# Expert stage of a two-block transformer on one core: norms applied after the up projection, fetched rows transposed later, loads ahead in whole tiles

## The chip, the core and the metric

The kernel runs on one core of a Trainium2 chip. TensorE (PE in the profile, its weight loads PEld) multiplies matrices, VectorE (DVE), ScalarE (ACT) and GpSimd (POOL) work on elements, and SyncE (SP) issues most of the DMAs; the five run beside one another and wait for each other through semaphores. The metric is the device time of one execution in microseconds, the median of the runs.

## The reference, cut to what matters

The program computes a whole small model on 512 tokens of width 1024 (first a block with two layers, then a second block). The change touches only its last part, the mixture of experts. There are 32 experts; a router gives each token two of them with a gate weight:

```python
def hier_moe(h, ...):                       # h = rmsnorm(x) * norm2_g
    ...
    gates = jnp.sum(jax.nn.one_hot(e_idx, N_EXPERTS) * e_weight[..., None], axis=1)
    ...
        a = jnp.einsum('nd,edf->nef', hf, w_g[sl])        # 1024 -> 256
        u = jnp.einsum('nd,edf->nef', hf, w_u[sl])        # 1024 -> 256
        hid = jax.nn.silu(a) * u * gates[:, sl, None]
        out = out + jnp.einsum('nef,efd->nd', hid, w_d[sl])   # 256 -> 1024
```

`rmsnorm(x, g) = x * rsqrt(mean(x*x) + eps) * g`. The factor `rsqrt(...)` is one number per token, so it can be multiplied onto the token's row, or onto `a` and `u`, with the same result.

## The kernel before, in words

All data are float32. A product is made of three (or, in the experts' up projection, of two stacked) matmuls over a high and a low part of each operand; so every weight tile that arrives (`wraw`, `h`, `xh`/`xl` or `t`, 128x1024, 0.5 MB) is split: ACT casts the high part (`whi`, L260), DVE subtracts (`wlo`, L261). Weights come in one stream of such tiles in the order of use, through SP's queue (`load` L254, `load_to` L235, `load_halves` L242).

**Expert stage (`moe`, from L1408).** The router ranks each token within its two experts; an expert has 64 slots (`CAP`). Six weight tiles belong to an expert: four for gate and up, two for down. Token rows, already times the norm's gain but without the token's norm factor, lie in DRAM (`xr`). Experts are taken in blocks of four (`EB`); `take(e)` prepares block e while block e-4 is computed:

- `onehot` (`oh`, DVE L1601), eight small matmuls (`slot_cols`, L1364) and some short DVE instructions (`slot_rows`) give for each slot the token's row number and norm factor; `sr` (L1378) is the cast of the row numbers to integers. Its tile has two buffers, and the row numbers of the block before the last are still read by that block's scatter.
- `rows_in` (L1392): two gathers by GpSimd fetch 128 rows each into `rows` (two tiles).
- L1474: GpSimd multiplies both tiles by the norm factors.
- `rows_turn`: PE transposes them (L1401), ACT and DVE split them into `xs` (L1404, L1405), which has two buffers.

For each expert `expert_up` runs 16 matmuls (L1618) with the rows' high and low parts stacked on the partitions, ACT copies the lower half (`low`, L1620) and one matmul with `fold` (L1626) adds it to the upper; `expert_hidden` takes the silu (`hid`, ACT L1628) and the product (DVE L1629). One expert later `expert_turn` transposes `hid` (L1638) and splits it (`hh`), and `expert_down` multiplies (L267 to L269) into two banks. After two experts `add_rows` applies the gates (`y`, ACT L1532 for one half, DVE L1533 for the other), and GpSimd scatters the rows with an adding DMA into the output (L1535).

`take` is a generator; the main loop advances it by `next(coming, None)`, once before the down projection and once after `expert_hidden` (twice in the first expert of a block). Where its `yield`s stand decides behind which expert's work an instruction is written. Within that the framework's scheduler places instructions on each engine; an engine executes in order, so what stands first and waits holds up what follows.

Loads ahead: tile j goes to one of 26 places (`AHEAD`), in turn: 9 `wraw` tiles (`RING`), 4 tiles of the finished activations (`h`), 8 pairs of half tiles `xh`, `xl`, and 5 pairs of `t`. A half tile pair is two DMAs and two splits.

```python
                n = j % AHEAD - RING
                ...
                    self.ahead[j] = self.load_halves(j, [self.p_x.tile([128, T], F32, name=t) for t in ("xh", "xl")])
```

Of the kernel before, what the change touches and what calls it, by code (L numbers as in the profile page):

```python
# [9 lines left out]
F32 = mybir.dt.float32  # L10
F32R = mybir.dt.float32r
I32 = mybir.dt.int32
U8 = mybir.dt.uint8
AF = mybir.ActivationFunctionType
OP = mybir.AluOpType
# [7 lines left out]
T = NM + S  # L23
H2 = T // 2
NT = S // 128
# [17 lines left out]
CAP = 64  # L43
EB = 4
# [9 lines left out]
RING = 9  # L54
AHEAD = RING + 17
# [146 lines left out]
class Ker:  # L202
# [252 lines left out]
        return rb[:, :n], y  # L455

    def xpair(self, n=T):
        return (self.p_x.tile([128, T], F32R, name="xh")[:, :n], self.p_x.tile([128, T], F32R, name="xl")[:, :n])

    def xsplit(self, h, gname, n=T, first=lambda k: None):  # L460

# [780 lines left out]
    def route_begin(self):  # L1242
        nc = self.nc
        rc = self.tmp()
        self.rc = [rc[:, 0:288].rearrange("p (a b) -> p a b", a=8), rc[:, 288:416], rc[:, 416:452], rc[:, 452:496]]
        for t, name in zip(self.rc, ("w_r", "tri", "b_r", "rdesc")):
            nc.gpsimd.dma_start(t, self.a[name])
        self.lgp = self.psb()
        zero = self.tmp(144)
        nc.vector.memset(zero, 0.0)  # L1250
        nc.tensor.matmul(self.lgp[:, :144], self.ident, zero, start=True, stop=False, skip_group_check=True)
        self.xt = {j: self.tmp(512) if n == 7 else self.p_x.tile([128, T], F32, name=("xh", "xl")[n % 2])[:, :512]
                   for n, j in enumerate(XORDER)}
        self.xr = self.p_d.tile([S, D], F32, name="xr")
        self.ss, self.nr = None, 0

# [151 lines left out]
    def moe(self):  # L1408
# [3 lines left out]
        with ExitStack() as es:  # L1412
# [5 lines left out]
            gcol = pk.tile([128, 4, NEXP // 2, 8], F32R, name="gcol")  # L1418
            nc.vector.memset(gcol.bitcast(F32), 0.0)
            self.xg = [pk.tile([128, D], F32, name=f"rows{n}") for n in range(EB // 2)]  # L1420
            for t in self.xg:
                nc.gpsimd.memset(t, 0.0)
            gall = pk.tile([128, 4, NEXP], F32, name="gall")
# [37 lines left out]
            def take(e):  # L1461
                n = EB // 2
                oh = self.onehot(pe, rank[:, :, e:e + EB], iota)
                s = self.slot_cols(pe, oh, gcol, e, n, 0, 8 if e else 4)
                r, y = self.slot_rows(pe, s, n)
                for b in range(n):
                    self.rows_in(b, r[:, b:b + 1])
                if e == 0:
                    self.gating(pr, found, gall, gcol)
                    s = self.slot_cols(pe, oh, gcol, e, n, 4, 8)  # L1470
                places[e] = r, self.slot_gates(pe, s)
                yield
                for b in range(n):
                    nc.gpsimd.tensor_scalar(self.xg[b], self.xg[b], y[:, b:b + 1], None, op0=OP.mult)  # L1474
                    yield
                for b in range(n):
                    yield from self.rows_turn(b, bufs(e)[0][:, :, 2 * b:2 * b + 2])

            def fetch(j):

                n = j % AHEAD - RING
                if n < 0:
                    self.ahead[j] = self.load(j)
                elif n < 4:
                    self.ahead[j] = self.load_to(j, self.hp[n])
                elif n < 12:
                    self.ahead[j] = self.load_halves(j, [self.p_x.tile([128, T], F32, name=t) for t in ("xh", "xl")])
                else:
                    self.ahead[j] = self.load_halves(j, [self.tmp(512), self.tmp(512)])

# [7 lines left out]
            for e in range(NEXP + 1):  # L1498
                if e % EB == 0:
                    list(coming)  # L1500
                    coming = take(e + EB) if e + EB < NEXP else iter(())
                if e < NEXP:
                    def hu(j, e=e):
                        if e * 6 + j not in self.ahead:
                            fetch(e * 6 + j)
                        return self.hu(idx=e * 6 + j)

                    x2, h2 = bufs(e)
                    up = self.expert_up(e % 2, x2, e % EB, hu, lambda: e and self.expert_turn(e % 2 == 0, *last))
                else:  # L1510
                    self.expert_turn(e % 2 == 0, *last)
                next(coming, None)
                if e > 0:
                    f = e - 1
                    if f % 2 == 0:
                        py = [self.psb(), self.psb()]
                    self.expert_down(py, f % 2 == 0, f % 2 == 1, *last)
                    if f % 2:
                        self.add_rows(pe, py, places[f // EB * EB], f % EB // 2, out)
                if e < NEXP:  # L1520
                    last = self.expert_hidden(e % 2, up), h2, hu
                for _ in range(2 if e % EB == 0 else 1):
                    next(coming, None)
            self.more_raw = None
# [2 lines left out]
    def add_rows(self, pe, py, place, b, out):  # L1527

        nc = self.nc
        r, g = place  # L1530
        y = pe.tile([128, D], F32, name="y")
        nc.scalar.activation(y[:, :512], py[0], AF.Copy, scale=g[:, b:b + 1])  # L1532
        nc.vector.tensor_scalar(y[:, 512:], py[1], g[:, b:b + 1], None, op0=OP.mult)  # L1533

        nc.gpsimd.indirect_dma_start(out=out[:S], out_offset=bass.IndirectOffsetOnAxis(ap=r[:, b:b + 1], axis=0), in_=y, in_offset=None,  # L1535
                                     bounds_check=S - 1, oob_is_err=False, compute_op=OP.add)

    def overflow(self, pe, cmax, rank, gall, gcol, xs, hh, out):
# [3 lines left out]
        with tc.If(cnt > CAP):  # L1542
# [5 lines left out]
            with tc.For_i(0, NEXP, 1) as e:  # L1548
                with tc.For_i(CAP, S, CAP) as b:
# [1 line left out]
                    nc.vector.memset(oh[:, :, CAP:2 * CAP].bitcast(F32), 0.0)  # L1551
                    r, y = self.slot_rows(pe, self.slot_cols(pe, oh, gcol, 0, 1, 0, 4), 1)
                    self.rows_in(0, r)
                    nc.gpsimd.tensor_scalar(self.xg[0], self.xg[0], y, None, op0=OP.mult)
                    list(self.rows_turn(0, xs[0][:, :, 0:2]))
                    hu = lambda j: self.hu(idx=e * 6 + j)
                    up = self.expert_hidden(0, self.expert_up(0, xs[0], 0, hu)), hh[:2], hu
                    self.expert_turn(False, *up)
                    py = [self.psb(), self.psb()]
                    self.expert_down(py, True, True, *up)  # L1560
# [34 lines left out]
    def onehot(self, pe, rank, iota):  # L1595

        nc = self.nc
        n = rank.shape[-1]
        m = n * CAP
        oh = pe.tile([128, NT, EB * CAP], F32R, name="oh", bufs=1)  # L1600
        nc.vector.tensor_tensor(oh[:, :, :m].rearrange("p a (e c) -> p a e c", e=n), iota[:, None, None, :].to_broadcast([128, NT, n, CAP]),  # L1601
                                rank[:, :, :, None].to_broadcast([128, NT, n, CAP]), op=OP.is_equal)
        return oh
# [16 lines left out]
        nc.scalar.copy(low[CAP:], pa[CAP:])  # L1620
        return pa, low

    def expert_hidden(self, par, up):
        nc = self.nc
        pa, low = up
        nc.tensor.matmul(pa, self.fold, low, start=False, stop=True, skip_group_check=True)  # L1626
        hid = self.hids[par]
        nc.scalar.activation(hid[:CAP], pa[:CAP, :256], AF.Silu)  # L1628
        nc.vector.tensor_mul(hid[:CAP], hid[:CAP], pa[:CAP, 256:])  # L1629
        return hid  # L1630

    def expert_turn(self, second, hid, hh, hu):
# [516 lines left out]
```

## Time and profile before

| | |
|---|---|
| runs (3) | median 1864.43 us, 1859.45 to 1865.34 |
| profiled execution | 1857.01 us, span 1855.2 us |
| PE busy in the span | 1694.2 us (91%), mean granted clock 0.956 |
| DVE, ACT, POOL busy | 1108.9, 844.4, 138.9 us |
| read from HBM | 221.89 MB |
| expert stage, first gather to the end | 1439.06 to 1855.2 us |

PE's share over the span is high because of the dense layers, which fill the first three quarters. The expert stage has other limits and is read by itself. In a timeline row the first number is the start in microseconds from the span's start, the second the time from the first start to the last end in the row; a bracket says how long the engine stood idle before and what ended it.

### The profile page before, as it was taken

Reading aid. Unit: us, or ns where it says so; the run is one execution under the profiler, and the core shown is the slowest. Engines: PE = TensorE matmul, PEld = TensorE weight load, DVE = VectorE, ACT = ScalarE, POOL = GpSimd, SP = SyncE. Lnnn points to the kernel's source line nnn. Section 1 sums busy time; section 2 is a strip of 40 time slices with the busy share of each in tenths; the row PEclk is TensorE's granted clock in tenths of the full one; section 3 lists DMA queues with packets and bytes.
Section 4 is the critical chain, followed back from the end, with each engine's and each line's share of the span. In section 5 each row is a group of like instructions: output and inputs, shape, how many; then the busy total and the mean of one; then the engine's idle time right before and its main releaser. Section 6 shows DMA issues by size and latency. Waiting matters only on the chain. (4 is left out here: it accounts for less than half of the span.)

```text
span 1855.2 us, 26474 instructions
## 1 busy us (share of the span) xinstructions
PE 1694.2 (91%) x10298; PEld 1459.3 (79%) x10298; DVE 1108.9 (60%) x1966; ACT 844.4 (46%) x1425; POOL 138.9 (7%) x99
## 2 busy tenths in 40 slices
PE   8999999999999999999999999999998566677766
PEld 8989999999999999788888886777777444555544
DVE  7667674534343445534343457997676567777766
ACT  5465553423232334413232335533634466676665
POOL 0000000000000000000000000000000424122222
PEclk9999999999999998999999999998999788998888
DMA  5211023222222221232332343121137688778771
GB/s 179 68 57 58 12 62 107 92 91 90 89 89 90 91 91 57 85 98 91 96 97 91 109 134 92 59 77 48 30 121 278 227 278 299 261 261 278 263 245 20
DMA packets 82418, 229.98 MB, mean 124 GB/s; under 512 B 11608, under 2 KB 11664, under 8 KB 82288
## 3 DMA queue, kind: packets, MB, share of 16 engines
q1 hardware_dynamic: 76752, 217.80, 35.3%
q0 software_dynamic: 5536, 10.45, 2.5%
q8 instruction: 82, 1.34, 0.3%
q14 instruction: 48, 0.39, 0.1%
HBM read 221.89 MB, written 14.69 MB: 128 GB/s over the span
## 5 line engine op out<-in xcount | busy, mean ns | idle before, releaser
L260 ACT CAST whi<-wraw 128x1024 fp32r<-128x1024 f32 (+1 forms) x271 | 281.9, 1044 | 626.3 <-PE pm L290 293.3
L261 DVE TENSOR_TENSOR wlo<-wraw,whi 128x1024 fp32r<-128x1024 f32 (+1 forms) x271 | 328.3, 1216 | 41.6 <-ACT whi L260 32.1
L290 PE MATMUL pm<-xh,whi 128*128 128x264 f32 x976 | 202.6, 289 | 8.9 <-ACT whi L260 6.0
L290 PE MATMUL pm<-xh,wlo 128*128 128x264 f32 x976 | 201.1, 287 | 0.0
L290 PE MATMUL pm<-xl,whi 128*128 128x264 f32 x976 | 200.9, 287 | 0.0
L290 PE MATMUL ps<-xh,whi 128*128 128x512 f32 x472 | 192.1, 407 | 0.0
L290 PE MATMUL ps<-xh,wlo 128*128 128x512 f32 x472 | 186.2, 395 | 0.0
L290 PE MATMUL ps<-xl,whi 128*128 128x512 f32 x472 | 185.5, 393 | 0.0
L290 PEld LDWEIGHTS pm<-xh,whi 128*128 128x128 f32 x976 | 153.2, 191 | 10.0 <-ACT whi L260 6.0
L290 PEld LDWEIGHTS pm<-xh,wlo 128*128 128x128 f32 x976 | 152.9, 190 | 0.1
L290 PEld LDWEIGHTS pm<-xl,whi 128*128 128x128 f32 x976 | 152.6, 190 | 0.4 <-DVE xl L468 0.3
L1618 PE MATMUL ps<-wlo,xs 128*128 128x512 f32 x256 | 110.7, 432 | 25.1 <-DVE wlo L261 24.5
L290 PEld LDWEIGHTS ps<-xh,whi 128*128 128x128 f32 x472 | 89.3, 189 | 23.7 <-issue 1.8
L1618 PE MATMUL ps<-whi,xs 128*128 128x512 f32 x256 | 106.0, 414 | 1.9 <-ACT whi L260 1.9
L290 PEld LDWEIGHTS ps<-xh,wlo 128*128 128x128 f32 x472 | 89.0, 189 | 21.0
L290 PEld LDWEIGHTS ps<-xl,whi 128*128 128x128 f32 x472 | 89.4, 189 | 19.5 <-issue 0.5
L290 PE MATMUL pm<-ah,whi 128*128 128x264 f32 x512 | 104.1, 284 | 0.0
L290 PE MATMUL pm<-ah,wlo 128*128 128x264 f32 x512 | 104.0, 285 | 0.0
L290 PE MATMUL pm<-al,whi 128*128 128x264 f32 x512 | 103.7, 284 | 0.0
L290 PE MATMUL ps<-ah,whi 128*128 128x512 f32 x256 | 101.1, 395 | 0.0
L290 PE MATMUL ps<-ah,wlo 128*128 128x512 f32 x256 | 101.0, 394 | 0.0
L290 PE MATMUL ps<-al,whi 128*128 128x512 f32 x256 | 100.5, 392 | 0.0
(499 smaller groups left out, 3277.6 us busy)
## 6 DMA issues: line engine op xcount, KB each, us to landing
wraw<-in_stream_dram SPq DMA_DIRECT2D x268, 512.0 KB, 3.5
t<-in_stream_dram SPq DMA_DIRECT2D x70, 256.0 KB, 5.5
h<-in_stream_dram SPq DMA_DIRECT2D x29, 512.0 KB, 5.5
xh<-in_stream_dram SPq DMA_DIRECT2D x56, 256.0 KB, 5.4
xl<-in_stream_dram SPq DMA_DIRECT2D x56, 256.0 KB, 5.5
h<-in_xT_dram SPq DMA_DIRECT2D x16, 264.0 KB, 3.5
hd<-h SPq DMA_DIRECT2D x8, 256.0 KB, 2.0
h<-hd SPq DMA_DIRECT2D x8, 256.0 KB, 3.5
```

The lines of the kernel that those rows point to most:

```text
L260: self.nc.scalar.copy(hi, src)
L261: i = self.nc.vector.tensor_sub(lo, src, hi.bitcast(F32))
L290: nc.tensor.matmul(ps, w[:, b, :], x[:, sl], start=(first and f and i == 0), stop=(last and l and i == nb - 1))
L1618: nc.tensor.matmul(pa, xk, v[:, k], start=kk == 0 and n == 0, stop=kk == 7 and n == 1, skip_group_check=True)
```

## The change

The scaling on GpSimd goes. The norm factor, brought to one column per expert (`sn`; for the second expert of a pair by eight narrow matmuls with the one-hot moved by 64 slots), becomes the scale of the silu and the scalar of the product. The transposes are written five yields behind the gathers in place of one yield and two scalings, so they stand in the third and fourth expert of the block before. Both halves of `y` are on ACT. `xh` and `xl` become the halves of one tile `xp`, into which a whole weight tile is loaded with one DMA; after the first 26 tiles the turn is over 21 places, without `t`. The one-hot tile moves to another pool.

```diff
     def xpair(self, n=T):
-        return (self.p_x.tile([128, T], F32R, name="xh")[:, :n], self.p_x.tile([128, T], F32R, name="xl")[:, :n])
+        t = self.p_x.tile([128, 2, T], F32R, name="xp")
+        return t[:, 0, :n], t[:, 1, :n]
...
             def take(e):
...
-                r, y = self.slot_rows(pe, s, n)
+                r, t = self.slot_rows(pe, s, n)
                 for b in range(n):
                     self.rows_in(b, r[:, b:b + 1])
+
+                y = pe.tile([128, EB], F32, name="sn")
+                y2 = y.rearrange("p (b two) -> p b two", two=2)
+                nc.vector.tensor_copy(y2[:, :, 0], t)
+                ps = self.psb()
+                for b in range(n):
+                    for i in range(NT):
+                        c = oh[:, i, b * 128 + CAP:min(b * 128 + CAP + 128, EB * CAP)]
+                        nc.tensor.matmul(ps[:c.shape[-1], b * 8:b * 8 + 4], c, gcol[:, i, e // 2 + b, :4],
+                                         start=i == 0, stop=i == NT - 1, skip_group_check=True)
+                s2 = pe.tile([128, n, 2], F32, name="sq")
+                nc.vector.tensor_copy(s2[:CAP], ps[:CAP, :n * 8].rearrange("p (a b) -> p a b", a=n)[:, :, 1:3])
+                nc.vector.tensor_add(y2[:CAP, :, 1], s2[:CAP, :, 0], s2[:CAP, :, 1])
...
-                yield
-                for b in range(n):
-                    nc.gpsimd.tensor_scalar(self.xg[b], self.xg[b], y[:, b:b + 1], None, op0=OP.mult)
+                places[e] = r, self.slot_gates(pe, s), y
+                for _ in range(5 if e else 1):
                     yield
                 for b in range(n):
                     yield from self.rows_turn(b, bufs(e)[0][:, :, 2 * b:2 * b + 2])
...
-                n = j % AHEAD - RING
+                n = (j if j < AHEAD else (j - AHEAD) % (AHEAD - 5)) - RING
...
                 elif n < 12:
-                    self.ahead[j] = self.load_halves(j, [self.p_x.tile([128, T], F32, name=t) for t in ("xh", "xl")])
+                    self.ahead[j] = self.load_to(j, self.p_x.tile([128, 2, T], F32, name="xp"))
...
     def add_rows(self, pe, py, place, b, out):
...
         nc.scalar.activation(y[:, :512], py[0], AF.Copy, scale=g[:, b:b + 1])
-        nc.vector.tensor_scalar(y[:, 512:], py[1], g[:, b:b + 1], None, op0=OP.mult)
+        nc.scalar.activation(y[:, 512:], py[1], AF.Copy, scale=g[:, b:b + 1])
...
-    def expert_hidden(self, par, up):
+    def expert_hidden(self, par, up, y):
...
-        nc.scalar.activation(hid[:CAP], pa[:CAP, :256], AF.Silu)
-        nc.vector.tensor_mul(hid[:CAP], hid[:CAP], pa[:CAP, 256:])
+        nc.scalar.activation(hid[:CAP], pa[:CAP, :256], AF.Silu, scale=y)
+        nc.vector.scalar_tensor_tensor(hid[:CAP], pa[:CAP, 256:], y, hid[:CAP], op0=OP.mult, op1=OP.mult)
```

What stands on the engines, at the border between the second and the third block (experts 8 and 9; `hid` of expert 8 and then of expert 9). DVE before, from the scatter's second `y` half to the first `xs` of the rows that `sr` names:

```order
L1533 TENSOR_SCALAR y<-ps,sg 128x512
L1629 TENSOR_TENSOR hid_13315<-hid_13315,ps 64x256
L1386 TENSOR_TENSOR sg<-sp 64x2 x2
L261 TENSOR_TENSOR wlo<-wraw,whi 128x1024
L261 TENSOR_TENSOR hh_13304<-ps,hh_13301 128x2x64
L261 TENSOR_TENSOR wlo<-wraw,whi 128x1024 x2
L1378 CAST sr<-st 128x2
L261 TENSOR_TENSOR wlo<-wraw,whi 128x1024 x3
L1629 TENSOR_TENSOR hid_13319<-hid_13319,ps 64x256
L1601 TENSOR_TENSOR oh<-iota,rank 128x1024
L1405 TENSOR_TENSOR xs_13306<-ps,xs_13306 128x4x2x64
```

DVE now, at the same border, from expert 8's `hid` to the first `xs`:

```order
L1645 SCALAR_TENSOR_TENSOR hid_13256<-ps,sn,hid_13256 64x256
L261 TENSOR_TENSOR wlo<-h_91,whi 128x1024
L261 TENSOR_TENSOR wlo<-h_92,whi 128x1024
L1382 CAST sr<-st 128x2
L261 TENSOR_TENSOR hh_13245<-ps,hh_13242 128x2x64
L261 TENSOR_TENSOR wlo<-wraw,whi 128x1024 x2
L261 TENSOR_TENSOR wlo<-xp,whi 128x1024 x3
L1645 SCALAR_TENSOR_TENSOR hid_13260<-ps,sn,hid_13260 64x256
L261 TENSOR_TENSOR wlo<-xp,whi 128x1024
L261 TENSOR_TENSOR wlo<-h_93,whi 128x1024
L261 TENSOR_TENSOR hh_13250<-ps,hh_13248 128x2x64
L1409 TENSOR_TENSOR xs_13247<-ps,xs_13247 128x4x2x64
```

`y` has left DVE, the one-hot has moved ahead of `sr` (just above the first row shown), and seven splits stand between `sr` and the first `xs`, where three stood.

PE before, at the same place: the last matmuls of expert 9's up projection, its `fold`, the transposes of the first fetched tile, then the down projection of expert 8 (`hh`):

```order
L1618 MATMUL ps<-whi,xs_13306 128x512
L1618 MATMUL ps<-wlo,xs_13306 128x512
L1626 MATMUL ps<-low_13318,fold 128x512
L1401 MATMUL ps<-c_97,rows_13295 128x128 x4
L267 MATMUL ps<-whi,hh_13301 128x512
L268 MATMUL ps<-wlo,hh_13301 128x512
L269 MATMUL ps<-whi,hh_13304 128x512
```

PE now, in the up projection of expert 10, behind the turn of expert 9 (L1654); the down projection of expert 8 lies further up:

```order
L1633 MATMUL ps<-wlo,xs_13244 128x512
L1654 MATMUL ps<-c_97,hid_13260 128x128 x2
L1633 MATMUL ps<-whi,xs_13244 128x512
L1405 MATMUL ps<-c_97,rows_13235 128x128 x4
L1633 MATMUL ps<-wlo,xs_13244 128x512
L1633 MATMUL ps<-whi,xs_13244 128x512
L1633 MATMUL ps<-wlo,xs_13244 128x512
L267 MATMUL ps<-whi,hh_13248 128x512 x2
```

The transposes have moved behind the down projection of expert 8 and half of expert 10's up projection.

What `sr` waits for is the same in both; DVE before, with waits (DMASW are the semaphores of the DMAs that GpSimd issues, DMAHW of those that SP issues):

```order
L261 TENSOR_TENSOR wlo<-wraw,whi 128x1024 [waits DMAHW2_49]
L261 TENSOR_TENSOR wlo<-wraw,whi 128x1024 [waits DMAHW3_49]
L1378 CAST sr<-st 128x2 [waits DMASW6_49,DMASW7_49,DMASW5_49,DMASW4_49]
L261 TENSOR_TENSOR wlo<-wraw,whi 128x1024 [waits DMAHW4_49,PE_49,Activation_49]
L261 TENSOR_TENSOR wlo<-wraw,whi 128x1024 [waits DMAHW5_49,PE_49,Activation_49]
```

In the changed program `sr` (L1382) waits for the same four semaphores; only its neighbours have moved.

## Rows read from the trace of the kernel before

**Rows 1.** The page's forty slices of the span (46.4 us each), busy tenths of PE and DMA.

```profile
PE   8999999999999999999999999999998566677766
...
DMA  5211023222222221232332343121137688778771
```

**Rows 2.** Windows of about one block, cut at the gathers: length, busy us (and instructions) of PE, PEld, DVE, ACT, POOL, granted clock, DMA share, GB/s.

```profile
1565.80:1617.10 51.30, 35.68 (x148) 26.06 (x148) 36.50 (x59) 32.89 (x55) 13.26 (x6) 0.87 0.76 256
...
1667.00:1719.00 52.00, 36.90 (x147) 27.06 (x147) 36.21 (x59) 31.05 (x53) 13.04 (x7) 0.83 0.83 278
1719.00:1771.80 52.80, 37.81 (x149) 27.37 (x149) 36.83 (x58) 32.64 (x54) 12.97 (x6) 0.82 0.76 252
```

**Rows 3.** Who waited for whom from 1400 to 1855 us: total, times, longest.

```profile
PE ps L1401 <- POOL rows L1474: 73.7, 9, 11.9
...
DVE xs L1405 <- ACT xs L1404: 52.9, 11, 11.4
...
DVE sr L1378 <- issue: 27.3, 6, 5.6
...
DVE wlo L261 <- ACT whi L260: 23.4, 19, 2.3
```

**Rows 4.** GpSimd in order of time.

```profile
1446.25 5.69 POOL L1474 TENSOR_SCALAR rows<-rows,sy 128x1024 f32<-128x1024 f32 x2 [4.70 <-DMA rows<-xr,sr]
...
1504.51 1.56 POOL L1535 DMA_INDIRECT out_dram<-y,sr  x1 [15.86 <-DVE sg L1386]
...
1538.10 10.00 POOL L1535 DMA_INDIRECT out_dram<-y,sr  x1 [12.89 <-ACT whi L260]
1556.09 2.47 POOL L1535 DMA_INDIRECT out_dram<-y,sr  x1 [7.99 <-DVE sg L1386]
...
1570.75 2.85 POOL L1474 TENSOR_SCALAR rows<-rows,sy 128x1024 f32<-128x1024 f32 x1 [1.43 <-DMA rows<-xr,sr]
1574.66 2.84 POOL L1474 TENSOR_SCALAR rows<-rows,sy 128x1024 f32<-128x1024 f32 x1 [1.06 <-DMA rows<-xr,sr]
1589.67 1.90 POOL L1535 DMA_INDIRECT out_dram<-y,sr  x1 [12.16 <-DVE xs L1405]
...
1812.90 2.25 POOL L1535 DMA_INDIRECT out_dram<-y,sr  x1 [15.92 <-ACT whi L260]
```

**Rows 5.** DVE in order of time.

```profile
1473.68 0.69 DVE L1405 TENSOR_TENSOR xs<-ps,xs 128x512 fp32r<-128x512 f32 x1 [4.55 <-ACT xs L1404]
...
1533.63 1.22 DVE L261 TENSOR_TENSOR wlo<-h,whi 128x1024 fp32r<-128x1024 f32 x1
1534.76 1.28 DVE L1405 TENSOR_TENSOR xs<-ps,xs 128x512 fp32r<-128x512 f32 x2
...
1541.10 0.68 DVE L261 TENSOR_TENSOR wlo<-xh,whi 128x512 fp32r<-128x512 f32 x1
1541.70 0.68 DVE L261 TENSOR_TENSOR wlo<-xl,whi 128x512 fp32r<-128x512 f32 x1
...
1554.54 0.75 DVE L1533 TENSOR_SCALAR y<-ps,sg 128x512 f32<-128x512 f32 x1
1555.21 0.41 DVE L1629 TENSOR_TENSOR hid<-hid,ps 64x256 f32<-64x256 f32 x1
...
1564.79 0.17 DVE L1378 CAST sr<-st 128x2 int32<-128x2 f32 x1 [4.98 <-issue]
...
1575.42 0.69 DVE L1405 TENSOR_TENSOR xs<-ps,xs 128x512 fp32r<-128x512 f32 x1 [5.55 <-ACT xs L1404]
1578.44 1.22 DVE L261 TENSOR_TENSOR wlo<-h,whi 128x1024 fp32r<-128x1024 f32 x1 [2.33 <-ACT whi L260]
1580.56 1.23 DVE L261 TENSOR_TENSOR wlo<-h,whi 128x1024 fp32r<-128x1024 f32 x1 [0.90 <-ACT whi L260]
...
1598.31 0.41 DVE L1629 TENSOR_TENSOR hid<-hid,ps 64x256 f32<-64x256 f32 x1 [0.29 <-ACT hid L1628]
...
1605.90 0.75 DVE L1533 TENSOR_SCALAR y<-ps,sg 128x512 f32<-128x512 f32 x1 [0.49 <-PE ps L269]
```

**Rows 6.** PE in order of time, at the stall.

```profile
1573.65 1.11 PE L1401 MATMUL ps<-c,rows 128*128 128x128 f32 x4 [10.77 <-POOL rows L1474]
```

**Rows 7.** Windows of 4 us, columns as in rows 2.

```profile
1572.00:1576.00 4.00, 2.35 (x8) 2.06 (x9) 0.58 (x1) 0.58 (x1) 2.94 (x2) 0.50 0.36 136
1576.00:1580.00 4.00, 4.00 (x16) 3.15 (x15) 1.33 (x2) 1.56 (x2) 1.51 (x1) 0.65 0.00 0
1580.00:1584.00 4.00, 4.00 (x22) 3.27 (x21) 3.44 (x5) 4.00 (x7) 0.00 (x0) 1.00 0.62 200
...
1604.00:1608.00 4.00, 3.20 (x14) 2.09 (x13) 3.47 (x7) 3.52 (x6) 0.56 (x1) 1.00 1.01 370
```

**Rows 8.** Groups of instructions by line: busy us, mean ns of one, idle before.

```profile
L1196 DVE SCALAR_TENSOR_TENSOR h<-ps,vecs,h 128x512 f32<-128x512 f32 x8 | 6.0, 745 | 6.6 <-PE ps L1193 6.6
...
L1532 ACT ACTIVATE y<-ps,sg 128x512 f32<-128x512 f32 x16 | 11.0, 688 | 2.7 <-PE ps L269 2.5
```

**Rows 9.** DMA issues by line, 1380 to 1855 us: count, size, median us to landing.

```profile
h<-in_stream_dram SPq DMA_DIRECT2D x29, 512.0 KB, 5.5
...
out_dram<-y,sr POOLq DMA_INDIRECT x16, 8.6
```

**Rows 10.** SP's queue, who it waited for, 1380 to 1855 us.

```profile
SPq L254 <- DVE wlo L261: 112.9, 42, 11.3
```

More of the change, by code (lines that the diff above doesn't have):

```diff
@@ L1251, in route_begin @@
         nc.tensor.matmul(self.lgp[:, :144], self.ident, zero, start=True, stop=False, skip_group_check=True)
-        self.xt = {j: self.tmp(512) if n == 7 else self.p_x.tile([128, T], F32, name=("xh", "xl")[n % 2])[:, :512]
-                   for n, j in enumerate(XORDER)}
+        self.xt = {}
+        for n, j in enumerate(XORDER):
+            if n % 2 == 0:
+                t = self.p_x.tile([128, 2, T], F32, name="xp")
+            self.xt[j] = t[:, n % 2, :512]
         self.xr = self.p_d.tile([S, D], F32, name="xr")
@@ L1420, in moe @@
             self.xg = [pk.tile([128, D], F32, name=f"rows{n}") for n in range(EB // 2)]
+            self.oh = pk.tile([128, NT, EB * CAP], F32R, name="oh")
             for t in self.xg:
@@ L1470, in take @@
                     s = self.slot_cols(pe, oh, gcol, e, n, 4, 8)
-                places[e] = r, self.slot_gates(pe, s)
-                yield
-                for b in range(n):
-                    nc.gpsimd.tensor_scalar(self.xg[b], self.xg[b], y[:, b:b + 1], None, op0=OP.mult)
+                places[e] = r, self.slot_gates(pe, s), y
+                for _ in range(5 if e else 1):
                     yield
@@ L1520, in moe @@
                 if e < NEXP:
-                    last = self.expert_hidden(e % 2, up), h2, hu
+                    last = self.expert_hidden(e % 2, up, places[e // EB * EB][2][:CAP, e % EB:e % EB + 1]), h2, hu
                 for _ in range(2 if e % EB == 0 else 1):
@@ L1529, in add_rows @@
         nc = self.nc
-        r, g = place
+        r, g, _ = place
         y = pe.tile([128, D], F32, name="y")
         nc.scalar.activation(y[:, :512], py[0], AF.Copy, scale=g[:, b:b + 1])
-        nc.vector.tensor_scalar(y[:, 512:], py[1], g[:, b:b + 1], None, op0=OP.mult)
+        nc.scalar.activation(y[:, 512:], py[1], AF.Copy, scale=g[:, b:b + 1])
         nc.gpsimd.indirect_dma_start(out=out[:S], out_offset=bass.IndirectOffsetOnAxis(ap=r[:, b:b + 1], axis=0), in_=y, in_offset=None,
@@ L1553, in overflow @@
                     self.rows_in(0, r)
-                    nc.gpsimd.tensor_scalar(self.xg[0], self.xg[0], y, None, op0=OP.mult)
                     list(self.rows_turn(0, xs[0][:, :, 0:2]))
                     hu = lambda j: self.hu(idx=e * 6 + j)
-                    up = self.expert_hidden(0, self.expert_up(0, xs[0], 0, hu)), hh[:2], hu
+                    up = self.expert_hidden(0, self.expert_up(0, xs[0], 0, hu), y[:CAP, 0:1]), hh[:2], hu
                     self.expert_turn(False, *up)
@@ L1599, in onehot @@
         m = n * CAP
-        oh = pe.tile([128, NT, EB * CAP], F32R, name="oh", bufs=1)
+        oh = self.oh
         nc.vector.tensor_tensor(oh[:, :, :m].rearrange("p a (e c) -> p a e c", e=n), iota[:, None, None, :].to_broadcast([128, NT, n, CAP]),
```

## The prediction

> **What bounds the kernel now.** I read first the forty slices of the page [rows 1]: the first 30 slices (to 1391 us) have PE at eight or nine tenths; from slice 32 on PE stands at five to seven tenths and DMA mostly at seven or eight. That last quarter is the expert stage, and it is all that the change touches: with the tiles' names set aside, the program's order on PE, DVE, ACT and POOL is the same before and after up to the router, so I book nothing for the rest. Next the windows, cut at the gathers [rows 2]: four experts (a block, one call of `take`) need about 51 us, in which DVE is busy 36 to 37 us. No engine is full, so something stalls all of them. The waits [rows 3] name it. PE stood 73.7 us in front of the transposes of fetched rows, waiting for GpSimd's scaling; behind PE stood ACT, and behind ACT's part of `xs` stood DVE, 52.9 us. A second wait is DVE's own: `sr`, the cast of the row numbers, 27.3 us in six places, which the profile puts down to no engine. A third is DVE after ACT's `whi`, 23.4 us.
>
> One block in order of time shows how they hang together. The scatter of the second pair of experts starts at 1556.09 [rows 4]. DVE stands 4.98 us before `sr`, which begins at 1564.79, so it had run until 1559.81 [rows 5]. The order says why: `sr` overwrites row numbers that an earlier scatter reads, so it waits for all four semaphores of GpSimd's DMA queue, and it goes on 8.70 us after that scatter began. The gathers follow; the scalings are at 1570.75 and 1574.66 [rows 4], PE's first transpose at 1573.65 after 10.77 us of idleness [rows 6], DVE's first `xs` after 5.55 us more [rows 5]. PE comes back with its clock at 0.50 to 0.65 of full speed (the 1.2 GHz level for most of that time), after it did next to nothing from 1563 on; it is at 1.00 again from 1580 [rows 7]. In between DVE waits 2.33 and 0.90 us for `whi`. From 1582 to 1608 DVE then has no gap over half a microsecond.
>
> So a block is DVE's work, 36.5 us, and about 14.5 us of stalls: 5.0 (`sr`) + 5.55 (`xs`) + 3.2 (`whi`) + 0.8 (0.3 before a `hid`, 0.5 before a `y` [rows 5]). Blocks measured between second scatters last (1812.90 - 1504.51) / 6 = 51.4 us [rows 4].
>
> **The change part by part.** *Scaling on GpSimd removed, transposes later.* On PE the transposes no longer follow directly on the `fold` of the second expert; they stand in the third expert, behind the second one's turn. On DVE there are then, between `sr` and the first `xs`, seven splits, one `hid` and two `hh`. A whole split starts 1.13 us after the one before it (1533.63 to 1534.76), a half 0.60 us (1541.10 to 1541.70) [rows 5]; so 7 x 1.13 + about 0.7 = 8.6 us, and PE reaches the transposes some 7 us after `sr`. The rows must be there by then. In the trace the first gather has landed when the first scaling starts, 1570.75, which is 5.96 us after `sr` began; the second at 1574.66, 9.9 us after [rows 4]. Its transposes come another expert later, some 15 us after `sr`. Both are in time, the first by about 1 us. The 5.55 us goes, and nothing that the trace shows is late in its place, except:
>
> *The wait of `sr` stays, and grows.* I place D at the end of the split that the second scatter's last matmuls need (1553.2). Before: `y` ready at D + 1.3 (1554.54), scatter at D + 2.9, `sr` free at D + 11.6; DVE had work until D + 6.6, stall 5.0. After: both halves of `y` are on ACT, one behind the other. ACT's half now takes 0.69 us [rows 8]; its second ends about 0.3 us later than DVE's did, so `sr` is free at D + 11.9. DVE's work between: four splits 4.5, the one-hot 1.1, `hid` 0.4, `sg` 0.2 = 6.2. Stall 5.7 us. Behind `sr` on DVE stand `hh` and all splits, and PE waits for those; PE's idleness here is 5 to 6 us in place of 10.8. Whether its clock falls in that time the trace does not show: the bounds are 0 and the 3.2 us of today. I take 2, nearer to the row that there is.
>
> *`y` from DVE to ACT.* Two per block, 0.67 us each between starts (1554.54 to 1555.21) [rows 5]: DVE -1.3. ACT +1.4, of about 33 us busy in a block [rows 2], hidden while DVE is the one that is waited for; were ACT the bound, it would cost 1.4.
>
> *Norms in silu and product.* The silu only gets a scale operand. The product becomes a scalar-tensor-tensor of 64x256 from PSUM. Two rows bound it: the same kind at 128x512 takes 745 ns [rows 8], a plain tensor-tensor 0.69 us (1473.68 [rows 5]). So between 0 and +0.06 us each, four per block: +0.24. The column `sn` costs three small DVE instructions per `take`, about 0.1 us each as the `st` and `sg` around them: +0.3; its eight narrow matmuls run on PE, which has slack here.
>
> *Whole tiles.* In a block about 12 of 24 loads came as two halves. 2 x 0.60 against 1.13 saves 0.07 us each: -0.8. ACT saves too, unseen. The queue of loads ahead becomes 21 tiles in place of 26. At one split each 1.4 us that is still some 30 us ahead, against a landing of 5.5 us [rows 9]; I book 0 and put the danger under the rivals.
>
> Sum for a block: 36.5 - 1.3 - 0.8 + 0.3 + 0.24 = 34.9 of work, + 5.7 + 2 + 0.8 = 43.4 us. Gain 8.0 us, six times: 48. The take of the first block has no earlier scatter to wait for and loses its scaling, its `xs` wait (4.55 us at 1473.68 [rows 5]) and some of the `whi` waits: 8. At the start both scalings (5.69 us from 1446.25 [rows 4]) go, and the transposes stand behind the first of them, 2.85 us: 3. The last block keeps only the work: 1. Total 60 us. The profiled execution took 1857.0 us (span 1855.2 and 1.8 around it); 1797 on its scale. The runs' median is 7.4 us above it, so 1864.4 - 60 = **1804 us**.
>
> A rule speaks against this. POOL's DMA issue at 1538.10 took 10.00 us and not the 1.9 to 2.5 of its neighbours, with DVE running splits without a gap [rows 4, 5]; at 1589.67 DVE was as full and the issue took 1.90. The Trainium skill (SBUF — State Buffer, the "DVE blocks DMA" trap under "SBUF: two separate sides") says that descriptors of a DMA issued from GpSimd cannot be written while DVE holds the port that both share, in its two-port modes; under "Who interferes with whom" it says that tensor-tensor has no such mode and that the descriptors were not seen to starve behind it. By the first sentence a DVE without pauses would make every scatter slow; by the second nothing changes. The two rows agree with the second in one case and leave the other open.
>
> **The rivals.** *A: the rows are still late.* The first gather has 1 us of margin. If it takes 9.9 us, as the second does, PE stops there again: +2.7 us, and the 3.2 us of slow clock comes back whole: 47.3 per block. Gain 4.1 x 6 + 8 = 33: 1831. For: DMA is busier. Against: it was already full when today's gathers ran (the row at 1604, just before the next block's gathers, has it at 1.01 [rows 7]).
>
> *B: the second scatter is slow*, 10 us to issue in place of 2. Then `sr` comes 8 us later, the block is 51.4 again, and only the first block and the start are gained: 1852. For: the row at 1538.10, and DMA will be fuller. Against: the median scatter lands after 8.6 us [rows 9], and the one at 1556.09 took 8.70 beside a full DMA.
>
> *C: more is hidden.* PE's clock does not fall and the small gaps close: 34.9 + 5.7 = 40.6 per block; 10.8 x 6 + 12 = 77: 1787. Below that stands DMA: a block moves some 14 MB (51.3 us x 256 GB/s, 52 x 278 [rows 2]) and a full stretch shows 370 GB/s, DMA busy 1.01 [rows 7]: 38 us, or 1864 - 13.4 x 6 - 12 = 1772.
>
> *D, slower: loads become the bound.* Five tiles fewer lie ahead, a load goes out only when a whole tile is free, and SP's queue is in order, so one late release holds all loads behind it. If the stream then runs no faster than its poorest block shows, 252 GB/s [rows 2], 14 MB take 55 us, +4 per block: 1864 + 24 - 4 = 1884. It decides below 14 MB / 51.4 us = 272 GB/s. Against: SP stood 112.9 us at one line alone waiting for DVE to free a tile [rows 10]; loads wait for compute, and DMA was empty at 1576 [rows 7].
>
> *E: nothing is moved.* The order excludes it.
>
> **How the numbers follow.** Forecast (43.4 +- 2 per block) 0.66, C 0.14, A 0.09, B 0.06, D 0.05. The range goes from just above what DMA allows (1775) to past A (1842); the forecast alone has 1792 to 1816. A measurement of this kernel tells about 0.3% (5.6 us) from no change. Faster 0.93, same 0.02 (what lies between B and D), slower 0.05.
>
> **What would show it.** In the profile after: no PE wait at the transposes over 2 us and no `xs` wait on DVE; `sr` waits of 5 to 7 us, now DVE's longest; blocks of 43 us between second scatters; DVE busy above 0.8 of a block; PE's clock still dipping once per block; SP still waiting for DVE. Wrong, if PE again waits at the transposes (A), if scatters take 10 us (B), or if ACT's `whi` waits for DMA (D).

## The result and the profile after

The changed kernel takes 1799.99 us (median of 4, 1795.87 to 1800.50), the kernel before 1863.18 (4 runs); the ratio is 0.9658, with a 95% interval of 0.9636 to 0.9680. The forecast was 1804. One of the four executions of the experiment with the kernel before and three `sr` buffers took 8975.67 us at a granted clock of 0.167 (its median among the other three is 1818.10 us), and its ratio leaves that one out.

The slices of the page, as in [rows 1] (45.0 us each): from slice 32 on PE stands mostly at eight tenths (seven and six in the last two slices) in place of five to seven, and DMA mostly at eight.

```profile
PE   8999999999999999999999999999999888888776
...
DMA  5212014232232222133332334222013797888882
```

GpSimd in order of time, as [rows 4]; L1551 is now the scatter, L1396 the gather. The scalings are gone.

```profile
1436.40 1.08 POOL L1396 DMA_INDIRECT rows<-xr,sr  x1 [48.58 <-DMA wraw<-in_stream_dram]
...
1491.76 1.55 POOL L1551 DMA_INDIRECT out_dram<-y,sr  x1 [17.24 <-ACT y L1549]
...
1537.37 1.56 POOL L1551 DMA_INDIRECT out_dram<-y,sr  x1 [17.83 <-ACT y L1549]
1546.26 1.46 POOL L1396 DMA_INDIRECT rows<-xr,sr  x1 [7.33 <-issue]
...
1755.95 1.57 POOL L1551 DMA_INDIRECT out_dram<-y,sr  x1 [18.14 <-ACT hh L260]
```

Between second scatters six blocks now last (1755.95 - 1491.76) / 6 = 44.03 us in place of 51.40. The whole gain of the span, 1855.2 - 1798.7 = 56.5, can be cut at these rows: the first gather comes 2.7 us earlier (1436.40 for 1439.06), from there to the second scatter of the first block 10.1 less (55.36 for 65.45), six blocks 44.2 less, and the end behind the last of them 0.5 more (42.75 for 42.3). The rest of the 63 us by the medians is that the profiled execution of before was a short one.

Windows from second scatter to second scatter, columns as in [rows 2]:

```profile
1537.37:1580.77 43.40, 36.04 (x157) 26.20 (x157) 35.07 (x48) 32.88 (x46) 6.86 (x5) 0.96 0.83 306
...
1625.06:1662.64 37.58, 33.56 (x154) 24.52 (x154) 35.28 (x47) 32.72 (x46) 6.87 (x5) 1.00 0.86 314
...
1708.82:1755.95 47.13, 36.14 (x141) 24.55 (x140) 33.53 (x40) 32.75 (x45) 6.44 (x4) 0.93 0.85 310
```

DVE's work is 35 us a block, as forecast (34.9). One block of 37.58 us stands among others of 43 to 47, and its PE clock is the only one at 1.00; why is seen on DVE. Who waited for whom from 1400 us, as [rows 3]:

```profile
DVE sr L1382 <- issue: 28.2, 6, 6.6
...
DVE wlo L261 <- ACT whi L260: 23.4, 36, 1.6
...
DVE xs L1409 <- ACT xs L1408: 9.5, 7, 6.5
PE ps L1405 <- DMA rows<-xr,sr: 8.7, 3, 7.6
```

PE's 73.7 us in front of the transposes are 8.7, of which 7.6 belong to the first block, where there is nothing else to do. DVE's 52.9 us before `xs` are 9.5. What is left is `sr`. DVE in order of time, with two of its six waits, and PE at the first transposes of the rows, to be set beside [rows 5] and [rows 6]:

```profile
1545.30 0.17 DVE L1382 CAST sr<-st 128x2 int32<-128x2 f32 x1 [3.96 <-issue]
...
1556.11 0.67 DVE L1409 TENSOR_TENSOR xs<-ps,xs 128x512 fp32r<-128x512 f32 x1
...
1629.88 0.17 DVE L1382 CAST sr<-st 128x2 int32<-128x2 f32 x1 [0.84 <-issue]
```

```profile
1554.65 0.60 PE L1405 MATMUL ps<-c,rows 128*128 128x128 f32 x4
```

PE comes to the transposes 9.35 us after `sr` and does not stop; the first `xs` on DVE has no idle time. The wait of 0.84 us is that of the block of 37.58 us: there `sr` went on 4.8 us after the scatter at 1625.06, elsewhere 7.9 (1545.30 - 1537.37) and more. These two scatters landed 4.7 and 7.8 us after their issue; each time `sr` began 0.1 us later, which shows what it waits for. The clock around such a wait, in windows of 4 us, as [rows 7]:

```profile
1541.00:1545.00 4.00, 1.63 (x7) 0.96 (x6) 0.34 (x1) 2.67 (x3) 0.00 (x0) 1.00 1.00 336
1545.00:1549.00 4.00, 2.15 (x5) 1.72 (x6) 3.70 (x5) 0.10 (x1) 2.43 (x2) 0.75 0.44 152
1549.00:1553.00 4.00, 4.00 (x16) 3.10 (x14) 2.18 (x3) 2.89 (x4) 0.97 (x1) 0.82 0.80 316
1553.00:1557.00 4.00, 3.94 (x21) 2.98 (x20) 4.00 (x7) 3.95 (x7) 0.00 (x0) 1.00 0.03 4
```

PE is behind DVE here (1.63 us of 4 busy), its clock falls to 0.75 and 0.82 (so to the 1.2 GHz level for part of the time), and it is back from 1553. Before, it was at 0.50 and 0.65 [rows 7].

### The profile page after: what moved, and what is told of

The parts are those of the page before. It is cut to its first block, busy times and chain, and to the rows that moved or that the text cites. A ratio compares the mean times of both kernels' runs of the same rounds, so it can differ in the third digit from the quotient of the medians.

```text
span 1798.7 us, 26185 instructions
## 1 busy us (share of the span) xinstructions
PE 1691.8 (94%) x10362; PEld 1455.0 (81%) x10362; DVE 1096.9 (61%) x1888; ACT 845.3 (47%) x1355; POOL 73.5 (4%) x83
## 5 line engine op out<-in xcount | busy, mean ns | idle before, releaser
L261 DVE TENSOR_TENSOR wlo<-wraw,whi 128x1024 fp32r<-128x1024 f32 (+1 forms) x280 | 338.6, 1215 | 38.0 <-ACT whi L260 27.7
L290 PE MATMUL pm<-xp,whi 128*128 128x264 f32 x1952 | 324.3, 287 | 8.5 <-ACT whi L260 6.0
L290 PE MATMUL ps<-xp,whi 128*128 128x512 f32 x944 | 300.2, 399 | 0.0
L290 PEld LDWEIGHTS pm<-xp,whi 128*128 128x128 f32 x1952 | 272.4, 190 | 10.1 <-ACT whi L260 6.0
L290 PEld LDWEIGHTS ps<-xp,whi 128*128 128x128 f32 x944 | 174.7, 189 | 43.6 <-issue 2.3
L290 PE MATMUL pm<-xp,wlo 128*128 128x264 f32 x976 | 199.2, 285 | 0.0
L290 PE MATMUL ps<-xp,wlo 128*128 128x512 f32 x472 | 186.6, 396 | 0.0
L290 PEld LDWEIGHTS pm<-xp,wlo 128*128 128x128 f32 x976 | 151.8, 189 | 0.2
L290 PEld LDWEIGHTS ps<-xp,wlo 128*128 128x128 f32 x472 | 88.8, 188 | 20.1
L261 DVE TENSOR_TENSOR wlo<-xp,whi 128x1024 fp32r<-128x1024 f32 x70 | 83.9, 1215 | 9.5 <-ACT whi L260 9.1
L1633 PEld LDWEIGHTS ps<-wlo,xs 128*128 128x128 f32 x256 | 48.3, 189 | 48.0 <-DVE wlo L261 39.9
```

Source lines behind the costliest of these rows:

```text
L261: i = self.nc.vector.tensor_sub(lo, src, hi.bitcast(F32))
L290: nc.tensor.matmul(ps, w[:, b, :], x[:, sl], start=(first and f and i == 0), stop=(last and l and i == nb - 1))
L1633: nc.tensor.matmul(pa, xk, v[:, k], start=kk == 0 and n == 0, stop=kk == 7 and n == 1, skip_group_check=True)
```

## The experiments

Each was timed beside the kernel before, on the same chip. The medians of the kernel before lie between 1858.1 and 1863.2 us, so differences between experiments below 5 us are read as nothing. Block lengths stand beside them; each is read from the one execution that was profiled.

**Lateness alone.** The kernel before, with two `yield`s more in front of the transposes.

```diff
+                for _ in range(2 if e else 0):
+                    yield
                 for b in range(n):
                     yield from self.rows_turn(b, bufs(e)[0][:, :, 2 * b:2 * b + 2])
```

> The kernel before with the transposes written two yields later, where the changed kernel has them; GpSimd still scales the rows, whole `y` and loads as before. My theory (the gain comes from PE no longer stopping in front of rows that are not ready): the first scaled tile is there about 8.8 us after `sr`, PE comes to it some 7 us after, so 2 of the 5.55 us before `xs` stay, and the slow clock is about 2 in place of 3.2; a block is some 46.5 us and the time 1863 - 4.9 x 6 = 1834 us, or less (down to 1820) if the wait goes wholly. Rival (the gain needs the scaling gone, as its 2.85 us are in the path of the rows wherever the transposes stand): within 10 us of the kernel before, 1853 to 1863.

Measured: 1830.93 us, ratio 0.9823 (0.9782 to 0.9865); blocks of 47.24 us. As my theory said, half of the gain. (The four runs spread from 1823.72 to 1835.64; the profiled one, 1834.94, is one of the two longer ones, so its blocks are rather long.) The two worst blocks had 50.5 and 51.2 us, and the longer one shows what still stands in front of the transposes; GpSimd, then DVE:

```profile
1609.97 1.38 POOL L1392 DMA_INDIRECT rows<-xr,sr  x1 [8.33 <-DVE wlo L261]
...
1616.67 4.44 POOL L1474 TENSOR_SCALAR rows<-rows,sy 128x1024 f32<-128x1024 f32 x1 [3.04 <-DMA rows<-xr,sr]
```

```profile
1622.93 0.69 DVE L1405 TENSOR_TENSOR xs<-ps,xs 128x512 fp32r<-128x512 f32 x1 [4.35 <-ACT xs L1404]
```

The scaling took 4.44 us and not 2.85; more on this below.

**Without the lateness.** The changed kernel with the transposes at the place of before:

```diff
-                for _ in range(5 if e else 1):
+                for _ in range(3 if e else 1):
                     yield
```

> The changed kernel with the transposes two yields earlier, at the place they had before; everything else of the change stays. My theory: PE stands in front of the fetched rows again, now for the gather alone (5.9 us after `sr` in place of 8.8), so `xs` waits 2.7 us and the clock drops for longer: 3 to 4 us per block, 1800 + 6 x 3.5 = 1821 us. Rival (taking the scaling off the path was enough, the place of the transposes does nothing): 1797 to 1803 us. Second rival (place is all): back to 50 us per block, 1836 us.

Measured: 1834.62 us, ratio 0.9859 (0.9827 to 0.9891); blocks of 48.73 us. The second rival's number: without the place, the change keeps 28 of 63 us. My theory had the direction and half of the size. It counted the first gather at 5.96 us after `sr`; here DVE

```profile
1553.06 0.17 DVE L1382 CAST sr<-st 128x2 int32<-128x2 f32 x1 [4.17 <-issue]
...
1562.10 0.69 DVE L1409 TENSOR_TENSOR xs<-ps,xs 128x512 fp32r<-128x512 f32 x1 [5.05 <-ACT xs L1408]
```

waits 5.05 us, hardly less than the 5.55 with the scaling, since PE got the rows 7.3 us after `sr` (its transposes began at 1560.36).

**The wait before `sr`.** One more buffer for the row numbers, in the changed kernel and in the one before:

```diff
-        r = pe.tile([128, EB // 2], I32, name="sr")[:, :n]
+        r = pe.tile([128, EB // 2], I32, name="sr", bufs=3)[:, :n]
```

> The changed kernel with three buffers in place of two for `sr`, the row numbers: its cast then no longer overwrites numbers that the scatter issued just before still reads. My theory (the wait before `sr`, 28.2 us in six places, is that and nothing else, and DVE is what is waited for around it): the wait goes, the PE clock no longer falls behind it, and a block is 39 to 40 us: 1800 - 6 x 4.5 = 1773 us. Rival (something else is late right behind: DMA, which already runs at 0.75 to 0.96, or the rows): 1785 to 1800 us, with the wait moved to `whi` after DMA or to the transposes.

Measured: 1765.55 us (1765.01 to 1766.01), ratio 0.9484 (0.9456 to 0.9513). This version beats both kernels, by 97 and 34 us. Its waits hold no `sr` any more, and a window of one block reads

```profile
1568.00:1605.70 37.70, 34.47 (x157) 24.93 (x156) 34.91 (x48) 32.85 (x46) 5.71 (x4) 1.00 1.00 379
```

with a PE clock of 1.00. Blocks last 38.17 us: 5.86 less for a wait of 4.7 (28.2 / 6). The excess, about 1.2 us a block, is spread over DVE's other waits (0.4 for `whi`, 0.3 for `hid`, 0.2 for `xs`) and a little work; that the slower clock behind the wait had made them is likely, but not shown by itself.

> The kernel before with three buffers for `sr`. My theory (the two stalls of a block are separate: one before `sr`, one in front of the transposes, which is counted from `sr`): the 27.3 us before `sr` go, the waits in front of the transposes stay, 1863 - 27 = 1836 us. Rival (both stalls hide the same DMA or PE time, so that one grows when the other goes): 1855 to 1863 us.

Measured: 1818.47 us, ratio 0.9762 (0.9723 to 0.9800); blocks of 44.00 us. More than expected, and neither theory: the stalls are not separate. Who waited for whom, from 1400 us:

```profile
PE ps L1401 <- POOL rows L1474: 47.2, 9, 11.3
...
DVE xs L1405 <- ACT xs L1404: 28.5, 7, 11.5
```

With `sr` issued early the gathers go out early as well, and the wait in front of the transposes falls too (52.9 to 28.5 us on DVE). One more buffer of 8 bytes a partition brought two thirds of what the change brings. (The gathers now go out just ahead of the second scatter, so its cut, and the 44.00, can be off by some us.)

**`y` back on DVE**, in the changed kernel and then together with three `sr` buffers:

```diff
-        nc.scalar.activation(y[:, 512:], py[1], AF.Copy, scale=g[:, b:b + 1])
+        nc.vector.tensor_scalar(y[:, 512:], py[1], g[:, b:b + 1], None, op0=OP.mult)
```

> The changed kernel with the second half of `y` back on DVE. My theory (DVE is what a block waits for, ACT has room): 1.3 us more DVE work per block less 0.3 us that the scatter, and with it `sr`, comes earlier: 1800 + 6 to 8 = 1806 us (1803 to 1809). Rival (the half is hidden, as the wait before `sr` takes up what DVE does before it): 1797 to 1802.

Measured: 1795.74 us, ratio 0.9663 (0.9637 to 0.9689), which is the change's own; blocks of 42.80 us. Who waited for whom, from 1400 us:

```profile
DVE sr L1382 <- issue: 19.2, 6, 5.6
DVE wlo L261 <- ACT whi L260: 14.1, 13, 1.6
```

The rival: DVE's wait before `sr` shrinks from 28.2 to 19.2 us, about as much as the work that came back (6 x 2 x 0.67 = 8). Its wait behind ACT's `whi` shrinks as well, from 23.4 to 14.1 us.

> The changed kernel with three `sr` buffers and the second half of `y` back on DVE. Taken by itself (e3_ydve) that half cost nothing, 1795.7 against 1800. My theory (there the wait before `sr` took it up; where no such wait is left, DVE's 1.3 us per block count): 1765.5 + 8 = 1773 us, 1770 to 1777. Rival (without the wait DMA is the bound, at 0.85 to 1.00 of its time, and DVE's work is hidden beside it): 1762 to 1768.

Measured: 1765.52 us, ratio 0.9496 (0.9461 to 0.9530); 38.23 us a block. The same as without, so my theory fell here too, although DVE is busy 1.1 us a block longer. Where that time comes from is seen in DVE's wait behind ACT, without the half on DVE and then with it, from 1400 us:

```profile
DVE wlo L261 <- ACT whi L260: 21.3, 36, 1.6
```

```profile
DVE wlo L261 <- ACT whi L260: 14.3, 16, 1.6
```

The wait is 7.0 us shorter, as much as the work that came back: with both halves of `y` on ACT, DVE spends the time that it saves waiting for ACT's `whi`. So the rival is right that the work is hidden, but beside ACT as far as these rows show. DMA ran at 0.87 to 1.00 in the blocks, but SP still waited for DVE to free tiles, so that DMA is the limit there is not shown.

**Loads.** First half tiles and 26 places as before (`xpair` and the router's tiles go back to `xh` and `xl` with it), then the second of these pieces alone:

```diff
-                    self.ahead[j] = self.load_to(j, self.p_x.tile([128, 2, T], F32, name="xp"))
+                    self.ahead[j] = self.load_halves(j, [self.p_x.tile([128, T], F32, name=t) for t in ("xh", "xl")])
...
-                n = (j if j < AHEAD else (j - AHEAD) % (AHEAD - 5)) - RING
+                n = j % AHEAD - RING
```

> The changed kernel with the loads ahead as before: half tiles `xh` and `xl` with two DMAs and two splits each, 26 places in turn. My theory (whole tiles save DVE 0.07 us a tile and ACT something): +0.8 us per block, 1805 us (1802 to 1809). Rival 1 (the five places fewer hold loads back, so that the older way is the faster one): below 1797. Rival 2 (half tiles cost ACT and the queues much more than DVE shows): over 1812.

> The changed kernel with whole tiles but with 26 places in turn to the end: the five pairs of `t` stay in use, each two DMAs and two splits. My theory (neither number of places is what holds loads): 5 of 26 tiles are halves again, +0.3 us per block, 1802 us (1798 to 1805). Rival (a queue that reaches five tiles further matters): 1790 or less.

Measured: 1808.21 us (ratio 0.9724, 0.9700 to 0.9748) with half tiles, blocks of 44.38; 1802.91 (0.9689, 0.9665 to 0.9712) with 26 places, blocks of 44.74. Both in the ranges of my theories. The 8 us of whole tiles are little more than the 5 us by which the kernel before varies, and the profiled executions (spans 1802.9 and 1798.7) are 4 us apart. The five places that were given up cost nothing that can be seen.

**Place and `sr` together.** Three `sr` buffers and the early place:

> The changed kernel with three `sr` buffers and with the transposes two yields earlier. My theory (the stall in front of the transposes and that before `sr` are separate, and the place of the transposes is worth the same in either; e2_early showed 34.6 us, of them about 4.7 us in each of six blocks): 1765.5 + 28 = 1794 us (1785 to 1800). Rival (with `sr` issued early there is enough work between it and the transposes that their place no longer matters): 1764 to 1770.

Measured: 1793.55 us, ratio 0.9636 (0.9616 to 0.9657). As expected. PE's line of waits in this kernel, and in that with three `sr` buffers and the late place:

```profile
PE ps L1405 <- DMA rows<-xr,sr: 34.8, 8, 7.8
```

```profile
PE ps L1405 <- DMA rows<-xr,sr: 7.5, 2, 7.2
```

PE stands 27.3 us longer in front of the rows, and the time is 28 us longer: the place keeps most of its worth where `sr` is early (34.6 us with two buffers). (Blocks are not given here: GpSimd issues the next gathers ahead of the second scatter, so that cuts at scatters shift.)

**The norms alone.** The kernel before with late transposes and whole tiles; only the scaling by GpSimd is left of it.

> The kernel before with the transposes two yields later and with whole tiles and 21 places; GpSimd still scales the rows and DVE still makes half of `y`. It differs from e3_ydve (1795.7 us) by the norms alone. My theory (the 2.85 us of a scaling lie in the path of the rows even at the later place, where 28 us of waiting before `xs` were left): 1831 - 8 for the tiles = 1823 us, 1816 to 1829, so that the norms are worth some 27 us. Rival (e1_late was slow for its half tiles, and late transposes with whole tiles give it all): below 1805.

Measured: 1809.71 us, ratio 0.9735 (0.9698 to 0.9772): between the two. Its blocks last 43.88 us, against 42.80 of the kernel with `y` back on DVE, which differs by the norms and by the place of the one-hot tile (its move to another pool was not tried by itself). So in a steady block, with late transposes and whole tiles, the scaling costs about 1.1 us. Where it costs is the start: from the first gather to the second scatter of the first block 63.95 us against 55.39, since the first block has no earlier one in which its rows could be turned. Half tiles go with a longer block where the scaling is late (47.24 for 43.88, 3.4 us, from a long execution of the first experiment), while they cost the changed kernel 0.35; why they cost more beside the scaling stays open.

**Later still.** As the first experiment, with four `yield`s more.

> The kernel before with the transposes four yields later, two more than in e1_late; scaling, `y` and loads as before. My theory (the scaling costs only by its latency in front of the transposes): a place one expert further back hides it, the waits of PE in front of the transposes fall from 28 us to under 10, and the time comes to 1808 to 1818 us. Rival 1 (the scaling costs in another way, by taking the memory port or GpSimd's time from scatter and gather): 1825 to 1835, as in e1_late. Rival 2 (so late the `xs` come too late for their own block): over 1840.

Measured: 1814.21 us, ratio 0.9753 (0.9714 to 0.9792); blocks of 45.24 us. In my theory's range. PE's waits in front of the transposes are 14.5 us, not under 10; 11.3 of them are at the start, and only 3.2 in all blocks behind it. But the scaling itself became long. The durations of the scalings in two stretches (min, median, max in ns, then the first and last start), and windows that lie inside of the first and the last of these three scalings:

```profile
L1474 POOL TENSOR_SCALAR rows<-rows,sy x1: 8630/8630/8630, 1605.3 to 1605.3; 128x1024 f32<-128x1024 f32 x1
...
L1474 POOL TENSOR_SCALAR rows<-rows,sy x2: 5582/6915/8248, 1650.3 to 1658.6; 128x1024 f32<-128x1024 f32 x2
```

```profile
1606.00:1609.00 3.00, 2.90 (x12) 2.05 (x13) 3.00 (x4) 2.29 (x4) 3.00 (x1) 1.00 1.03 415
1609.00:1612.00 3.00, 3.00 (x15) 2.41 (x14) 2.95 (x5) 2.93 (x7) 3.00 (x1) 1.00 1.03 415
...
1661.00:1664.00 3.00, 1.90 (x11) 1.34 (x9) 3.00 (x4) 2.95 (x5) 3.00 (x1) 1.00 0.04 15
```

The same two views of the kernel before:

```profile
L1474 POOL TENSOR_SCALAR rows<-rows,sy x16: 2835/2848/3266, 1446.3 to 1780.8; 128x1024 f32<-128x1024 f32 x16
```

```profile
1570.75:1573.60 2.85, 0.00 (x0) 0.00 (x0) 0.00 (x0) 0.00 (x0) 2.85 (x1) 0.50 0.81 309
```

In the kernel before the scaling of the first tile ran in the stall in front of the transposes, with DVE, ACT and PE idle (0.00 us of 2.85), and took 2.85 us. Moved beside a DVE that is busy 3.00 of 3 us it took 8.63. ACT and PE are busy there too; two scalings of the kernel before with three `sr` buffers tell the engines apart. The first took 4.03 us, the second 2.83:

```profile
1646.66:1650.67 4.01, 0.00 (x0) 0.00 (x0) 1.31 (x3) 0.00 (x0) 4.01 (x1) 0.54 1.04 336
1605.66:1608.48 2.82, 2.76 (x9) 2.27 (x10) 0.10 (x1) 1.16 (x2) 2.82 (x2) 0.50 1.01 388
```

Beside 1.31 us of DVE's splits alone, PE and ACT idle, the scaling is 1.2 us longer; beside PE and ACT, with next to nothing on DVE, it is not, and DMA is full in both.

**The scaling off the path.** The changed kernel with the multiplications put back into spare tiles that nobody reads:

```diff
-                for _ in range(5 if e else 1):
+                for k in range(5 if e else 1):
                     yield
+                    if e and k < 2:
+                        for m in range(2):
+                            nc.gpsimd.tensor_scalar(self.tmp(512), self.xg[k][:, 512 * m:512 * m + 512], t[:, k:k + 1], None, op0=OP.mult)
```

> The changed kernel (1800 us) with the multiplications put back on GpSimd from the second block on, but into spare tiles that nobody reads: the same elements behind the same gathers (four of 128x512 per take), and nothing waits for them but the next gather. It does work that the reference does not need; its output is unchanged. In the kernels with late transposes the scaling took 2.85 us where DVE stood idle and 4 to 14 us beside a busy DVE. My theory (DVE is not held up by it; the scaling costs only where PE waits for its result): 1798 to 1804 us, the multiplications again 3 us and more a pair. Rival (both engines slow each other, so that GpSimd's work costs even off the path): 1808 us or more, with DVE's splits longer than 1.22 us beside it.

Measured: 1801.25 us, ratio 0.9678 (0.9654 to 0.9702); blocks of 44.12 us against 44.03. As my theory said: GpSimd's work costs nothing that can be seen here, where nothing waits for it, though half a tile took 1.6 to 6.0 us, and the splits of `xp` hardly changed on average (mean 1231 ns, 1215 in the changed kernel). (The "4 to 14 us" of the expectation are not one measure: 13.82 us was a pair, 8.63 the longest single scaling; and some beside a busy DVE took 2.85.) GpSimd's durations, and that group of DVE:

```profile
L1494 POOL TENSOR_SCALAR t<-rows,sy x28: 1557/2423/6006, 1476.0 to 1732.5; 128x512 f32<-128x512 f32 x28
```

```profile
L261 DVE TENSOR_TENSOR wlo<-xp,whi 128x1024 fp32r<-128x1024 f32 x46 | 56.0, 1231 | 6.3 <-ACT whi L260 6.1
```

## Why the prediction was right, point by point

- *What bounds it*: right. The stall in front of the transposes went, and with it the deeper dip of the clock. The sum of its parts was 60 us; by the cuts of the span it was 3 for the start (2.7 measured), 8 for the first block (10.1), 48 for six blocks (44.2) and 1 for the last (-0.5). That the errors partly cancel is luck.
- *"The 5.55 us goes, and nothing that the trace shows is late in its place"*: right, with a margin that varies. The gathers land later than before (median 7.7 us for 6.2). In the block shown PE comes to the transposes 9.35 us after `sr`, not 7, some 2 us after the rows; in the last two blocks it waits 0.2 and 0.9 us for them. Rival A is out; the changed kernel's wait for rows is 1.1 us outside the first block. (Its sum leaves out the 4 us of start and end that B and C count.)
- *Its parts were one sum in the prediction*; the runs divide it. The place is the greater part, 4.7 us of a block (48.73 to 44.03). The scaling is worth 1.1 us of a block once the place and whole tiles are there, and most of the first block's 10 us.
- *A block's terms*, over the six blocks: DVE's work 34.9 us as forecast, `sr` 4.7 for 5.7, waits for `whi` 3.1 for 2, the rest 1.4 for 0.8. The block came out 0.6 us from the forecast (44.03 for 43.4), in part by luck, as these errors offset each other.
- *"The wait of `sr` stays, and grows"*: stays, yes; it hardly grows: 4.7 us a block on average for 4.55 before (27.3 / 6), and 5.5 without the one block whose scatter landed after 4.7 us. Three of the six waits lie in the 5 to 7 us that were named as a sign. (1554.54, which the working calls ready, is where `y` begins on DVE; the sum goes by the scatter's start and does not hang on it.)
- *The clock, 2 us a block*: near, but not shown by itself. Behind the wait of the block shown the clock dips, as booked. But the 2 us were read off the waits for `whi`, and most of these are not the clock's: with three `sr` buffers, the clock at 1.00 in four of six blocks, DVE still waits 2.7 us a block for `whi`. Three `sr` buffers give 1.2 us beyond the wait; the one block without a wait is shorter than the mean of the other five (45.3) by 7.7 us, of which the wait explains (27.4 / 5 - 0.84) = 4.6, so 3.1 are left. The clock's share lies within these differences.
- *"`y` from DVE to ACT: DVE -1.3"*: the term that failed. DVE's work became less, but the time did not. The prediction had ACT's 1.4 us hidden while DVE is waited for; the runs show DVE waiting for ACT instead: its waits for `whi` are 9.3 us (23.4 for 14.1) and, without the `sr` wait, 7.0 us longer with both halves on ACT. Without this term the block would have been forecast at 44.7; 44.03 was measured.
- *Whole tiles, -0.8 us a block*: 8 us by the medians, 4 by the profiled executions, of which the blocks show 0.35 each; small, as said. *Rival D*, the fewer places, is out: 26 places are no faster.
- *Rival B*: no scatter of the changed kernel took over 2.1 us to issue, though DVE was busy 1.55 of the 1.56 us at 1537.37 (9.86 of 10.00 at 1538.10 in [rows 4]). Issues of 7 to 10 us were seen in the kernel before and in four experiments made from it, and in none made from the changed kernel, the one with multiplications on GpSimd included; what makes them stays open.

## What to carry to other kernels

For a wait that the profile puts down to no engine, ask what the waiting instruction would overwrite: here a third buffer for a tile of two numbers per partition was worth 34 us in one kernel and 44 in the other. Where a consumer waits for a DMA that takes several microseconds, first write it behind enough other work to cover that: here the place was worth 4.7 us of a block, the shorter path 1.1. Work that is moved from one engine to another counts only where the first does not wait afterwards, for the same thing or for the second engine; here it counted for nothing.

## What the runs showed of the hardware

An elementwise GpSimd instruction of 128x1024 in float32 took 2.85 us beside an idle DVE, and up to 8.63 us beside a DVE full of subtractions with two operands in SBUF. In the last experiment those of `xp` were longer by about 1% on average; single ones were held up too, by up to 0.35 us there (1.57 for 1.22) and 0.9 in the first experiment (2.08). The Trainium skill (SBUF — State Buffer, "Who interferes with whom") says that a DVE instruction with two SBUF inputs contends with a GpSimd instruction that reads SBUF. The trace agrees as far as it goes: in one of the windows (1661 to 1664 us) DMA was at 0.04 of its time, so that DMA does not explain the scaling of 5.58 us, and DVE was busy throughout; the scaling of 4.03 us beside DVE alone leaves PE and ACT out. The prediction weighed the same section for the scatters alone and passed over this sentence; it changed no term, as the changed kernel has no scaling. But it is one reason why two yields did not hide the scaling in the first experiment (4.44 us where PE then waited); with four, little of PE's wait was left in spite of it.
